# More up-projection pairs by seven products, and a longer plan, in a two-layer transformer trunk

## The chip, the core and the metric

The kernel runs on one core of one Trainium2 chip. A core has TensorE (PE in the profile; PEld is its weight load), VectorE (DVE), ScalarE (ACT), GpSimd (POOL) and SyncE (SP), which here only starts DMAs. Results of matmuls land in PSUM, which has eight banks of 128 partitions x 512 fp32 values; everything else lies in SBUF. GpSimd works on SBUF alone. The metric is the device time of one execution in microseconds (us).

## The reference

Two layers work on 512 tokens of width 1024 in fp32. Layer 0 mixes tokens by attention, layer 1 by a short convolution. Both go on with the same squared-ReLU MLP (hidden width 4096) and a gated embedding:

```python
for i in range(DEPTH):                                   # DEPTH = 2
    hn = rmsnorm(x, g[0])
    m = fox_attention(hn, ...) if i % 2 == 0 else short_conv(hn, ...)
    x = x + rmsnorm(m, g[1])
    h = rmsnorm(x, g[2])
    f = jnp.square(jax.nn.relu(h @ w_mlp_up[i])) @ w_mlp_down[i]
    x = x + rmsnorm(f, g[3])
    gate = jax.nn.sigmoid(rmsnorm(x, g[4]) @ w_ple_gate[i])
    x = x + rmsnorm((p[i] @ w_ple_proj[i]) * gate, g[5])
```

## The kernel before

**fp32 products.** Each operand is split into a high part (rounded to the matmul type, a cast on ACT) and a low part (value minus high part, a subtraction on DVE or POOL). `mm3` makes one product of three matmuls, high x high, low x high and high x low, at lines 420 to 422. A 512-column product is thus three matmuls of 512 columns. Of a weight tile `raw` the parts are named `wh` and `wl`.

**The MLP** (`mlp`) walks over eight groups of 512 hidden units. In each group four up-projections of 128 units (two *pairs*) are followed by a down-projection. Groups 0 to 6 do the down-projection by Strassen's scheme: a 2 x 2 block product by seven products instead of eight (`PRODUCTS`, in the order `STEPS`). Its operands are quarters of the activations (`A11`, `A12`, `A22` and the sums `S1` to `S4`, which POOL forms as tiles `s`) and quarters of the weights (`B11`, `B21`, `B22` and the sums `T1` to `T4`, tiles `dn_T`). Seven sums `acc` are carried over the groups, each group adding its products to them (`acc<-dn,acc`), and are combined after group 6. Group 7 has a plain down-projection.

**Up-projections by seven.** The pairs listed in `UP_SEVENS` use the same scheme, with 256-column matmuls: seven products of 12 matmuls (84) in place of 48 matmuls of 512 columns. They need sums of tokens (`T1` to `T4`, from the whole tokens `B..f`, once per layer), sums of weights (`up_S`, formed on POOL) and sums of the products (`d`, `v`, `m` on DVE). In the kernel before, these are the first pairs of groups 3 to 6.

**What sets the order.** Groups 1 to 6 of each MLP are laid out by a planner, `planned`: each step is put on an `Agenda` with an engine, a cost, what it follows, and the rooms it takes (raw weight buffers, banks). PE's order is written down; for ACT, DVE and POOL `emit` takes the ready step with the earliest due time, and the result is kept as the engines' order. Steps marked `shared` are planned one after the other with POOL's. Weights of a matmul may be split `LOOK` = 14 us before their use. Group 0, group 7 and everything outside the MLP are written as plain code (`up`, `down`, `combine`), weights being split some tiles ahead by `prepare`, and a scheduler orders them. Of the eight banks the planner gives 3 to the weight sums `dn_T` and 5 to products. The helper `add` at line 1208 issues all planned sums and low parts, so most DVE and POOL rows carry that line; line 1515 is the cast of a weight's high part.

Of the kernel before, what the change touches and what calls it, by code (L numbers as in the profile page):

```python
# [41 lines left out]
UP_SEVENS = [(gr, 0) for gr in range(3, 7)]  # L42
UP_FORMS = ("A11", "S2", "S1", "S3", "A12", "S4", "A22")
UP_PRODUCTS = (
    ("A11", "B11", "c", 0), ("S2", "T2", "a", 1), ("S1", "T1", "b", 0), ("S3", "T3", "b", 1),
    ("A12", "B21", "a", 0), ("S4", "B22", "c", 0), ("A22", "T4", "c", 1),
)
EXTRA = 7
LOOK = 14.0
LOOK_SUMS = 20.0  # L50
SUM_BANKS = 3
HOP = 0.25
MARGIN = 2.0
TOKENS_AT = 8.0
# [8 lines left out]
BANKED = range(1, 7)  # L63
# [17 lines left out]
low_on_pool = lambda key: key[0] == "up"  # L81


class Step:


    def __init__(self, engine, cost, run, after, begin, due, takes, uses, shared):
        self.engine, self.cost, self.run, self.shared = engine, cost, run, shared
        self.after, self.begin, self.due = list(after), begin, due
        self.takes, self.uses = takes, uses  # L90
        self.end = None


class Agenda:
# [5 lines left out]
    def add(self, engine, n, run, after=(), begin=0.0, due=1e9, takes=(), uses=(),  # L100
            shared=None):
# [3 lines left out]
                    engine == "POOL" if shared is None else shared)  # L105
# [5 lines left out]
    def emit(self):  # L111
# [8 lines left out]
        def room_for(step):  # L120
# [3 lines left out]
            for kind, n in need.items():  # L124
                left = self.rooms[kind] - n
# [56 lines left out]
def trunk(ctx: ExitStack, tc, x, xT, pT, g, gT, wv, wqk, bf, wo, wci, wcq, cw, wco, wup, wdn, wpp, wpg, out):  # L182
# [313 lines left out]
    def pre_norm(t, xs, gB, hT, name, also=lambda t, n, ps: None):  # L496
# [9 lines left out]

        put_off(t, turn)
# [601 lines left out]
    def mlp(l, hT, xs, then, late):  # L1109
# [72 lines left out]
        def planned(groups):  # L1182

            L, R, both = slice(0, S // 2), slice(S // 2, S), slice(0, S)
            agenda = Agenda({"raw": RAWS, "sum": SUM_BANKS, "ps": 8 - SUM_BANKS})
            first = begun[0]
            last = where["up", l, 14, 0] + SOON
# [10 lines left out]
            def act(n, run, after, uses=()):  # L1198
                return agenda.add("ACT", n, run, after, uses=uses)

            def dve(n, run, after, uses=(), due=1e9, shared=False):
                return agenda.add("DVE", n, run, after, uses=uses, due=due, shared=shared)
# [14 lines left out]

            def tokens_of_sevens():

                full = {}  # L1220
                for q in range(2):
                    for name in ("B11", "B12", "B22", "B21"):
# [8 lines left out]
                        full[name, q, 0] = gps(S, whole, (), begin=TOKENS_AT)  # L1231
                    for name, a, b in (("T1", "B12", "B11"), ("T2", "B22", "T1"),
                                       ("T3", "B22", "B12"), ("T4", "B21", "T2")):

                        def minus(name=name, q=q, a=a, b=b):
# [5 lines left out]
                        step = gps(S, minus, (full[a, q, 0], full[b, q, 0]))  # L1241
                        full[name, q, 0] = step
                        hi = act(S, lambda name=name, q=q: nc.scalar.copy(
                            T[name, q].hi[:, both], full[name, q][:, both]), (step,))
# [3 lines left out]
                            shared=True)  # L1248
# [10 lines left out]
            def part(gr, f, names, src, after, A):  # L1259
# [12 lines left out]
                step = dve(w, low, (act(w, high, (after,)),), shared=True)  # L1272
                for name in names:
                    low_of[gr, name, f // 2] = step

            def crossed(gr, f, q, at, A):

                d, m = (lambda: q["d"]), (lambda: q["m"])
                part(gr, f, ("A11", "A22"), lambda: q["d"][:, both], at["d"], A)
                part(gr, f, ("A12",), lambda: q["m"][:, R], at["m"], A)  # L1280
                sums(gr, f, q, at,
                     lambda: (q["m"][:, L], q["d"][:, R], q["d"][:, L], q["m"][:, R]), A)

            def sums(gr, f, q, at, of, A):
# [19 lines left out]
                a = gps(256, s12a, (at["d"], at["m"]))  # L1304
                b = gps(256, s12b, (a,))
                c = gps(256, s34a, (at["d"], at["m"]))
                e = gps(256, s34b, (b, c))
                part(gr, f, ("S1", "S2"), lambda: q["s12"][:, both], b, A)
                part(gr, f, ("S3", "S4"), lambda: q["s34"][:, both], e, A)

            def squared(gr, f, q, name, src, after, uses=()):

                def relu():
                    q["r" + name] = page(f"r{name}{l}_{gr}_{f}")
                    nc.scalar.activation(q["r" + name][:, both], src(), AF.Relu)
# [245 lines left out]
        def done(f, lo, hi, r):  # L1561
# [8 lines left out]
            if f == LATE:  # L1570
                gB.extend(late())
# [256 lines left out]
```

## Time and profile before

| | |
|---|---|
| median of 3 runs | 1214.74 us (1214.14 to 1214.89) |
| the profiled execution: time | 1214.68 us |
| its span, first to last instruction | 1212.9 us |
| granted TensorE clock | 0.999 |
| MLP of layer 0 / layer 1 in the span | 251.5 to 582.5 us / 817.7 to 1148 us |
| group 3 of layer 0 | 379 to 419 us |

The page's first part gives the busy time of each engine; the windows give the same for a stretch of the span, with the number of instructions behind x. In the views by group of instructions, "out<-in" names what is written and read, then come the count, the busy time, the mean duration of one in ns, and the engine's idle time ahead of them with what ended it. The chain of waits lists what released what, back from the last instruction: start, length, engine and line. PE's ends are modelled, so the pace of matmuls is read from starts.

### The profile page before, as it was taken

To read this page: it belongs to the slowest core of one execution; us is meant where nothing else is said; L and a number is where in the kernel's file an instruction comes from. 1 tells how busy PE (TensorE), PEld (TensorE's weight loads), DVE (VectorE), ACT (ScalarE), POOL (GpSimd) and SP (SyncE) were. 2 spreads that over 40 slices of the span, in tenths; PEclk is the share of its full clock that TensorE was granted. 3 is DMA by queue.
4 is the path that set the end of the run, shared out by engine and by line. 5 is a ranking of instruction groups with operands and counts; after the bars stand their busy time and mean duration, and the time that the engine had idled before them with its cause. 6 is when DMAs were issued, how large, how long until landed. Compare 5 with 4: busy or idle time off the path is not lost.

```text
span 1212.9 us, 19192 instructions
## 1 busy us (share of the span) xinstructions
PE 1201.4 (99%) x6463; PEld 1035.3 (85%) x6463; DVE 992.4 (82%) x1634; ACT 709.8 (59%) x1513; POOL 625.6 (52%) x592
## 2 busy tenths in 40 slices
PE   9999999999999999999999999999999999999997
PEld 7888887898888888888889999989888888888886
DVE  7888889584999999977877888766599999987773
ACT  7687778458664565445666533545757455663551
POOL 2035667155876765583213355226787567649110
PEclk9999999999999999999999999999999999999999
DMA  9475544623324333365223123542333334346301
GB/s 329 127 208 171 169 144 129 217 89 101 99 97 113 122 96 113 105 194 197 81 87 112 32 82 105 164 166 71 105 122 87 96 122 125 93 122 216 97 15 56
DMA packets 87316, 150.87 MB, mean 124 GB/s; under 512 B 10352, under 2 KB 18080, under 8 KB 87216
## 3 DMA queue, kind: packets, MB, share of 16 engines
q1 hardware_dynamic: 86640, 149.11, 39.5%
q8 instruction: 51, 0.84, 0.3%
q10 hardware_dynamic: 576, 0.53, 0.1%
q14 instruction: 49, 0.40, 0.1%
HBM read 139.03 MB, written 6.37 MB: 120 GB/s over the span
## 4 chain that ended last, share of the span: by engine, by line
PE 90%; DVE 3%; issue 2%; ACT 2%; POOL 1%; DMA 1%; SPq 0%; POOLq 0%; DVEq 0%; ACTq 0%
PE dn L420 8%; PE dn L422 8%; PE dn L421 8%; PE up L421 6%; PE up L420 6%; PE up L422 6%; PE v L628 3%; PE qk L420 2%; PE qk L422 2%; PE qk L421 2%; PE pg L420 2%; PE pg L421 2%; PE pg L422 2%; PE pT L742 1%; PE co L422 1%
## 5 line engine op out<-in xcount | busy, mean ns | idle before, releaser
L420 PE MATMUL up<-hTh,wh 128*128 128x512 f32 (+1 forms) x448 | 160.7, 359 | 0.0
L421 PE MATMUL up<-hTh,wl 128*128 128x512 f32 (+1 forms) x448 | 160.5, 359 | 0.0
L422 PE MATMUL up<-hTl,wh 128*128 128x512 f32 (+1 forms) x448 | 159.8, 359 | 0.0
L1208 POOL TENSOR_TENSOR wl<-raw,wh 128x512 fp32r<-128x512 f32 x88 | 137.6, 1590 | 27.0 <-ACT wh L1515 25.3
L429 DVE TENSOR_TENSOR wl<-raw,wh 128x512 fp32r<-128x512 f32 x162 | 140.5, 908 | 11.2 <-ACT wh L428 10.6
L1208 DVE TENSOR_TENSOR acc<-dn,acc 128x512 f32<-128x512 f32 x168 | 108.1, 679 | 6.4 <-PE dn L422 6.3
L428 ACT CAST wh<-raw 128x512 fp32r<-128x512 f32 x178 | 100.5, 628 | 4.5 <-DVE xd L525 4.4
L1515 ACT CAST wh<-raw 128x512 fp32r<-128x512 f32 x160 | 94.0, 620 | 2.4 <-DVE S3l L1208 2.4
L420 PEld LDWEIGHTS up<-hTh,wh 128*128 128x128 f32 x448 | 84.6, 189 | 12.4
L421 PEld LDWEIGHTS up<-hTh,wl 128*128 128x128 f32 x448 | 84.7, 189 | 12.1
L422 PEld LDWEIGHTS up<-hTl,wh 128*128 128x128 f32 x448 | 84.3, 189 | 12.6
L1515 ACT CAST wh<-dn_T 128x512 fp32r<-128x512 f32 x96 | 55.7, 585 | 64.3 <-DVE dn_T L1208 63.4
L1208 DVE TENSOR_TENSOR wl<-raw,wh 128x512 fp32r<-128x512 f32 x72 | 71.8, 1009 | 0.0
L1208 DVE TENSOR_TENSOR wl<-dn_T,wh 128x512 fp32r<-128x512 f32 x96 | 63.2, 680 | 1.4 <-ACT wh L1515 1.3
L1208 POOL TENSOR_TENSOR s<-qm,qd 128x256 f32<-128x256 f32 x8 | 6.9, 862 | 90.4 <-ACT qm L1319 71.1
L422 PE MATMUL qk<-hTl,wh 128*128 128x512 f32 x128 | 50.6, 396 | 0.0
L421 PE MATMUL pg<-wh,hTl 128*128 128x512 f32 x128 | 50.5, 394 | 0.0
L420 PE MATMUL pg<-wh,hTh 128*128 128x512 f32 x128 | 50.4, 394 | 0.0
L420 PE MATMUL qk<-hTh,wh 128*128 128x512 f32 x128 | 50.3, 393 | 0.0
L421 PE MATMUL qk<-hTh,wl 128*128 128x512 f32 x128 | 50.2, 392 | 0.0
L422 PE MATMUL pg<-wl,hTh 128*128 128x512 f32 x128 | 50.2, 392 | 0.0
L422 PE MATMUL dn<-wl,S3h 128*128 128x512 f32 x112 | 43.9, 392 | 0.1
(502 smaller groups left out, 4014.9 us busy)
## 6 DMA issues: line engine op xcount, KB each, us to landing
raw<-in_wup SPq DMA_DIRECT2D x128, 256.0 KB, 2.8
raw<-in_wdn SPq DMA_DIRECT2D x128, 256.0 KB, 2.7
raw<-in_wcq SPq DMA_DIRECT2D x36, 256.0 KB, 2.7
raw<-in_wqk SPq DMA_DIRECT2D x32, 256.0 KB, 5.3
raw<-in_wpg SPq DMA_DIRECT2D x32, 256.0 KB, 3.5
g<-in_g SPq DMA_DIRECT2D x22, 256.0 KB, 5.3
prl<-neg_c SPq DMA_DIRECT2D x16, 256.0 KB, 6.2
raw<-in_wo SPq DMA_DIRECT2D x16, 256.0 KB, 5.0
```

The lines of the kernel that those rows point to most:

```text
L420: nc.tensor.matmul(ps, a.hi, b.hi, start=start, stop=False)
L421: nc.tensor.matmul(ps, a.lo, b.hi, start=False, stop=False)
L422: nc.tensor.matmul(ps, a.hi, b.lo, start=False, stop=stop)
L428: nc.scalar.copy(hi, src)
L429: return eng.tensor_tensor(out=lo, in0=src, in1=hi.bitcast(F32), op=ALU.subtract)
L628: nc.tensor.matmul(ps[:, : V_CHUNKS[c][1]], getattr(of_x(k, t), p), getattr(ready["v", c, k], of), start=k == 0 and p == of, stop=k == KT ...
L742: nc.tensor.transpose(ps[:, b * P : (b + 1) * P], probs[h][b][:, j * P : (j + 1) * P], ident)
L1208: eng.tensor_tensor(out=out, in0=x, in1=y, op=op)
L1515: nc.scalar.copy(ready[key].hi[:, both], src())
```

## The change

1. `UP_SEVENS` lists both pairs of groups 2 to 6: ten pairs per layer by seven products, where there were four. The order of the seven products is A11, S2, A12, S1, S3, S4, A22.
2. The planner covers group 0, groups 1 to 6, the up-projections of group 7, and the splitting of all weights up to the gate's (`last` = four tiles before `pg`). `up_first` writes group 0 (for the first 128 units of each half of the tokens all matmuls with the tokens' high parts come first), `combined` puts the combining sums on POOL, `last_up` writes group 7's up-projections. Group 0's weight sums `dn_T` are formed on DVE in banks, where POOL formed them in SBUF.
3. For the weights of the down-projections and the sums `up_S` (`BESIDE`), ACT casts the value a second time, into a bank (`wb`). The low part is then the value minus `wb`, and no longer the value minus `wh`. 180 low parts read a bank so; the ACT casts grow by as many.
4. The products of a down-projection come in the order 1, 4, 2, 5, 6, 7, 3 (`TURNS`), no longer 1, 2, 4, 5, 6, 7, 3. Banks: 4 for weight sums and `wb` together, 4 for products. The planner also counts SBUF pages, and lets at most `IN_FLIGHT` = 14 split weights wait for PE.
5. The second pairs of groups 1 to 6 (where they go by seven) rectify and square the left half of `d` before the right half is there. Squares overwrite what they square.
6. `late`, the load of the residual and two gains, is issued 16 us of the plan before the down-projection of group 7.

The core of the diff:

```diff
-UP_SEVENS = [(gr, 0) for gr in range(3, 7)]
-UP_FORMS = ("A11", "S2", "S1", "S3", "A12", "S4", "A22")
+UP_SEVENS = [(gr, i) for gr in range(2, 7) for i in range(2)]
+UP_FORMS = ("A11", "S2", "A12", "S1", "S3", "S4", "A22")
...
+QUIET = 10.0
+IN_FLIGHT = 14
-SUM_BANKS = 3
+SUM_BANKS = 4
+APART_FROM = (1,)
+TURNS = (
+    (1, 0), (1, 1), (4, 0), (4, 1), (2, 0), (2, 1), (5, 0), (5, 1), (6, 0), (6, 1), (7, 0), (7, 1),
+    (3, 0), (3, 1),
+)
+BESIDE = ('dn', 'up_sum')
-TOKENS_AT = 8.0
+TOKENS_AT = 14.0
-BANKED = range(1, 7)
+BANKED = range(7)
...
-            last = where["up", l, 14, 0] + SOON
+            last = where["pg", l, 0, 0] + MORE
...
+                if i in APART_FROM and gr < 7:
+                    at["dl"] = squared(gr, f, q, "d", lambda: q["xd"], d, of=L)
+                    at["d"] = squared(gr, f, q, "d", lambda: q["xd"], e, of=R)
...
+                        def highs_first(ps=ps, of=of, weight=weight, f=f):
+                            ps.append(bank(f"up{l}_0_{f}{of.start}"))
+                            for k in range(KT):
+                                for part in ("hi", "lo"):
+                                    nc.tensor.matmul(
+                                        ps[0][:, L], weight(part, k), hT.hi[:, k, of],
+                                        start=k == 0 and part == "hi", stop=False,
+                                    )
...
+            up_first(A)
             tokens_of_sevens()
-            for gr in groups:
+            down_planned(0, A)
+            for gr in range(1, 7):
                 A = {}
                 for i in range(2):
                     (up_sevens if (gr, i) in UP_SEVENS else up_plain)(gr, i, A)
                 down_planned(gr, A)
+            combined()
+            blocks = [last_up(i) for i in range(2)]
...
+                def second_high(src=src, n=n, aside=aside):
+                    aside.append(bank(f"wb{n}"))
+                    nc.scalar.copy(aside[0].bitcast(F32R), src())
+
-                def low(key=key, src=src, eng=nc.gpsimd if plain_up else nc.vector):
-                    add(ready[key].lo[:, both], src(), ready[key].hi[:, both].bitcast(F32),
-                        ALU.subtract, eng)
+                def low(key=key, src=src, eng=nc.gpsimd if plain_up else nc.vector, aside=aside):
+                    of = aside[0] if aside else ready[key].hi[:, both].bitcast(F32)
+                    add(ready[key].lo[:, both], src(), of, ALU.subtract, eng)
...
+                if kind in BESIDE:
+                    hi = agenda.add("ACT", S, second_high, [hi], begin[0],
+                                    uses=uses, takes=[("sum", ("b", key))])
...
-                                         shared=not (of[0] == "dn" and isinstance(at, tuple)))
+                                         shared=kind != "dn_sum" and kind not in BESIDE)
```

**PE, the first pair of group 2 in layer 0.** `up0_2_0` is the bank of its first 128 units, `up0_2_0c` and `up0_2_0a` are banks of the pair by seven; `hTh` and `hTl` are the tokens' parts, `T2h` and `T2l` those of a token sum. Before:

```order
L420 MATMUL up0_2_0_4776<-hTh_87,wh113_4623 128x512
L421 MATMUL up0_2_0_4776<-hTh_87,wl113_4624 128x512
L422 MATMUL up0_2_0_4776<-hTl_88,wh113_4623 128x512
L420 MATMUL up0_2_0_4776<-hTh_87,wh113_4623 128x512
L421 MATMUL up0_2_0_4776<-hTh_87,wl113_4624 128x512
L422 MATMUL up0_2_0_4776<-hTl_88,wh113_4623 128x512
L420 MATMUL up0_2_0_4776<-hTh_87,wh114_4640 128x512
L421 MATMUL up0_2_0_4776<-hTh_87,wl114_4641 128x512
L422 MATMUL up0_2_0_4776<-hTl_88,wh114_4640 128x512
```

Now (the end of the first product and the start of the second, then the start of the third):

```order
L433 MATMUL up0_2_0c_4834<-hTh_87,wh112_4699 128x256
L434 MATMUL up0_2_0c_4834<-hTh_87,wl112_4700 128x256
L435 MATMUL up0_2_0c_4834<-hTl_88,wh112_4699 128x256
L433 MATMUL up0_2_0a_4857<-T2h0_0_4328,wh113_4826 128x256
L434 MATMUL up0_2_0a_4857<-T2h0_0_4328,wl113_4827 128x256
L435 MATMUL up0_2_0a_4857<-T2l0_0_4329,wh113_4826 128x256
L433 MATMUL up0_2_0a_4857<-hTh_87,wh114_4731 128x256
L434 MATMUL up0_2_0a_4857<-hTh_87,wl114_4732 128x256
L435 MATMUL up0_2_0a_4857<-hTl_88,wh114_4731 128x256
```

A weight tile served twelve matmuls of 512 columns, six for each of the pair's two blocks of units; now each of seven weight tiles serves twelve of 256 columns.

**DVE, the down-projection of group 3 in layer 0**, from the additions of its first product (`dn0_3_10`: product 1). Before:

```order
L1208 TENSOR_TENSOR acc0_1_0_4137<-dn0_3_10_5489,acc0_1_0_4137 128x512
L1208 TENSOR_TENSOR acc0_1_1_4139<-dn0_3_11_5490,acc0_1_1_4139 128x512
L1208 TENSOR_TENSOR dn_0_3_T3_0_5556<-dn_0_3_T2_0_5369,raw124_4970 128x512
L1208 TENSOR_TENSOR acc0_2_0_4163<-dn0_3_20_5520,acc0_2_0_4163 128x512
L1208 TENSOR_TENSOR acc0_2_1_4165<-dn0_3_21_5521,acc0_2_1_4165 128x512
L1208 TENSOR_TENSOR S1l0_3_2_5559<-s120_3_2_5518,S1h0_3_2_5558 128x512
L1208 TENSOR_TENSOR dn_0_3_T3_1_5584<-dn_0_3_T2_1_5454,raw126_5033 128x512
L1208 TENSOR_TENSOR acc0_4_0_4189<-dn0_3_40_5548,acc0_4_0_4189 128x512
L1208 TENSOR_TENSOR acc0_4_1_4191<-dn0_3_41_5549,acc0_4_1_4191 128x512
L1208 TENSOR_TENSOR wl154_5563<-dn_0_3_T3_0_5556,wh154_5562 128x512
L1208 TENSOR_TENSOR wl155_5599<-dn_0_3_T3_1_5584,wh155_5598 128x512
```

Now:

```order
L1243 TENSOR_TENSOR acc0_1_0_4174<-dn0_3_10_5739,acc0_1_0_4174 128x512
L1243 TENSOR_TENSOR acc0_1_1_4177<-dn0_3_11_5740,acc0_1_1_4177 128x512
L1243 TENSOR_TENSOR wl163_5735<-dn_0_3_T3_0_5685,wh163_5734 128x512
L1243 TENSOR_TENSOR A12l0_3_2_5791<-m0_3_1_5747,A12h0_3_2_5790 128x256
L1243 TENSOR_TENSOR S3l0_3_0_5751<-s340_3_0_5676,S3h0_3_0_5750 128x512
L1243 TENSOR_TENSOR acc0_4_0_4223<-dn0_3_40_5774,acc0_4_0_4223 128x512
L1243 TENSOR_TENSOR acc0_4_1_4232<-dn0_3_41_5775,acc0_4_1_4232 128x512
L1243 TENSOR_TENSOR S1l0_3_2_5826<-s120_3_2_5787,S1h0_3_2_5825 128x512
L1243 TENSOR_TENSOR acc0_2_0_4254<-dn0_3_20_5811,acc0_2_0_4254 128x512
L1243 TENSOR_TENSOR acc0_2_1_4258<-dn0_3_21_5812,acc0_2_1_4258 128x512
L1243 TENSOR_TENSOR wl164_5803<-dn_0_3_T3_1_5771,wh164_5802 128x512
L1243 TENSOR_TENSOR S3l0_3_2_5838<-s340_3_2_5799,S3h0_3_2_5837 128x512
```

Behind the additions of product 1 stand three instructions where one stood. Between the next pairs of additions stand one and two, where there were two and two. The products come in another order (1, 4, 2 where it was 1, 2, 4).

**POOL, group 0 of layer 0.** `s120` and `s340` are the sums `S1`/`S2` and `S3`/`S4` of a pair, `dn_0_0_T..` weight sums, `B..f` and `T..f` tokens and token sums. Before:

```order
L305 TENSOR_TENSOR dn_0_0_T1_1_3780<-raw81_3766,raw77_3758 128x512
L305 TENSOR_TENSOR dn_0_0_T3_1_3782<-raw83_3770,raw81_3766 128x512
L305 TENSOR_TENSOR dn_0_0_T2_1_3784<-raw83_3770,dn_0_0_T1_1_3780 128x512
L305 TENSOR_TENSOR dn_0_0_T4_1_3786<-raw79_3762,dn_0_0_T2_1_3784 128x512
L1141 TENSOR_TENSOR s340_0_0_3995<-q0_0_0_3751 128x256
L1141 TENSOR_TENSOR s120_0_1_4029<-q0_0_0_3751,q0_0_1_3752 128x256
L1141 TENSOR_TENSOR s120_0_1_4029<-s120_0_1_4029,q0_0_0_3751 128x256
L1141 TENSOR_TENSOR s340_0_0_3995<-q0_0_1_3752,s120_0_1_4029 128x256
L1141 TENSOR_TENSOR s340_0_2_4069<-q0_0_2_3753 128x256
L1141 TENSOR_TENSOR s120_0_3_4103<-q0_0_2_3753,q0_0_3_3754 128x256
L1141 TENSOR_TENSOR s120_0_3_4103<-s120_0_3_4103,q0_0_2_3753 128x256
L1141 TENSOR_TENSOR s340_0_2_4069<-q0_0_3_3754,s120_0_3_4103 128x256
```

Now:

```order
L1243 TENSOR_TENSOR B22f0_0_4043<-hTh_87,hTl_88 128x512
L1243 TENSOR_TENSOR T1f0_0_4068<-B12f0_0_3939,B11f0_0_3972 128x512
L1243 TENSOR_TENSOR s120_0_0_4091<-ql0_0_0_3793,qr0_0_1_3831 128x256
L1243 TENSOR_TENSOR s340_0_0_4111<-ql0_0_0_3793 128x256
L1243 TENSOR_TENSOR s120_0_0_4091<-s120_0_0_4091,ql0_0_0_3793 128x256
L1243 TENSOR_TENSOR B22f0_1_4136<-hTh_87,hTl_88 128x512
L1243 TENSOR_TENSOR s340_0_0_4111<-qr0_0_1_3831,s120_0_0_4091 128x256
L1243 TENSOR_TENSOR s120_0_2_4172<-ql0_0_2_3863,qr0_0_3_3965 128x256
L1243 TENSOR_TENSOR s340_0_2_4182<-ql0_0_2_3863 128x256
L1243 TENSOR_TENSOR s120_0_2_4172<-s120_0_2_4172,ql0_0_2_3863 128x256
L1243 TENSOR_TENSOR T1f0_1_4205<-B12f0_1_3990,B11f0_1_4012 128x512
L1243 TENSOR_TENSOR s340_0_2_4182<-qr0_0_3_3965,s120_0_2_4172 128x256
```

The weight sums of group 0 have left this queue, and token sums, which stood behind group 0's `s` sums, stand before and between them.

397 lines of the change are left out of this document (282 added, 115 removed).

## The prediction, blind

> **What bounds the kernel now.** I read the page's engine shares and its chain first, then the windows by group of the first MLP (with the sum line of the second), then a short window and two lines of the chain inside a group, to see what one matmul costs.
>
> ```profile
> span 1212.9 us, 19192 instructions
> PE 1201.4 (99%) x6463; PEld 1035.3 (85%) x6463; DVE 992.4 (82%) x1634; ACT 709.8 (59%) x1513; POOL 625.6 (52%) x592
> PE 90%; DVE 3%; issue 2%; ACT 2%; POOL 1%; DMA 1%; SPq 0%; POOLq 0%; DVEq 0%; ACTq 0%
> ```
> ```profile
> core 0: us, PE busy (x) PEld busy (x) DVE busy (x) ACT busy (x) POOL busy (x), PEclk, DMA share, GB/s
> 251.50:296.50 45.00, 44.84 (x294) 40.30 (x293) 28.85 (x37) 29.47 (x67) 25.16 (x25) 1.00 0.22 69
> 296.50:338.00 41.50, 41.45 (x182) 33.70 (x181) 34.32 (x41) 26.34 (x50) 38.13 (x31) 1.00 0.39 117
> 338.00:379.00 41.00, 41.00 (x182) 33.72 (x181) 40.65 (x53) 24.85 (x46) 34.71 (x26) 1.00 0.37 114
> 379.00:419.00 40.00, 40.00 (x218) 34.83 (x217) 39.03 (x56) 22.49 (x43) 25.94 (x21) 1.00 0.35 106
> 419.00:459.00 40.00, 40.00 (x218) 34.84 (x218) 39.14 (x57) 23.13 (x43) 24.54 (x19) 1.00 0.36 109
> ...
> 539.00:582.50 43.50, 43.50 (x194) 36.03 (x193) 30.95 (x42) 21.09 (x43) 19.70 (x18) 1.00 0.61 203
> sum 331.00, PE 330.79 PEld 283.09 DVE 285.55 ACT 191.01 POOL 217.90; mean PE 41.35 PEld 35.39 DVE 35.69 ACT 23.88 POOL 27.24
> ...
> sum 330.30, PE 330.27 PEld 283.15 DVE 284.21 ACT 190.32 POOL 217.95; mean PE 41.28 PEld 35.39 DVE 35.53 ACT 23.79 POOL 27.24
> ```
> ```profile
> 379.20:388.20 9.00, 9.00 (x77) 9.00 (x77) 8.18 (x13) 3.04 (x6) 3.21 (x2) 1.00 0.29 90
> ...
> 379.92 0.12 PE up_0c L422
> 337.27 0.23 PE dn L420
> 247.87 0.87 PE n_p L489 x8
> ```
> TensorE is the bound: 90% of the chain, at a granted clock of 1.00. A busy PE need not be a fast one, so its pace has to be checked. Inside a pair by seven products, 9.00 us hold 75 whole matmuls (77 less the two that the edges cut): 0.120 us from start to start at 256 columns, as in the chain. At 512 columns the chain has 0.23; closer, a group of one seven pair, one plain pair and its down-projection recurs every 40.0 us (379, 419, 459), and 40.0 - 84 x 0.120 = 29.9 us over 48 + 84 matmuls is 0.2267 us. So groups 3 and 4 are matmuls at full pace and nothing else: PE waits for nobody there, although DVE is busy 39.0 and 39.1 of 40.0 us. A whole MLP needs 192 x 0.12 (up, group 0) + 10 x 10.88 (plain pairs) + 4 x 10.08 (seven pairs) + 7 x 84 x 0.2267 (down) + 96 x 0.2267 (last down) + 16 x 0.11 (transposes) = 329.0 us, and takes 331.0 and 330.3. All that waiting could give back there is 3.3 us over both layers.
>
> **The change, part by part.**
>
> *Pairs by seven.* Four pairs per layer become ten, 12 more in all. A plain pair is 48 x 0.2267 = 10.88 us of PE, a seven pair 84 x 0.120 = 10.08 us: 0.80 us each, 12 x 0.80 = 9.6 us, all of it on the path. This is the main term. A rule speaks against it: the Trainium skill (TensorE: Matmul & The Clock Gate, Back-to-back issue gap) gives sustained spacings of about 81 ns at 128 columns and 131 ns at 512; an estimate half-way along for 256 columns is 98 ns, by which 84 short matmuls outlast 48 long ones and the change would cost some 23 us. The trace disagrees where it can be compared: 227 ns at 512 columns.
>
> *What DVE must do for it.* The order of the changed program has these DVE instructions from the first `acc` addition of one group to that of the next (512 columns / 256 columns): 52/3 from group 1 to 2, then 57/6, 55/6, 55/6, 52/6. Today it is 53/3 from group 3 to 4. The prices:
>
> ```profile
> L1208 DVE TENSOR_TENSOR acc<-dn,acc 128x512 f32<-128x512 f32 x74 | 47.7, 679 | 3.2 <-PE dn L422 3.2
> L1208 DVE TENSOR_TENSOR wl<-raw,wh 128x512 fp32r<-128x512 f32 x30 | 27.3, 917 | 0.0
> L1208 DVE TENSOR_TENSOR wl<-dn_T,wh 128x512 fp32r<-128x512 f32 x40 | 26.3, 680 | 0.7 <-ACT wh L1515 0.7
> L1208 DVE TENSOR_TENSOR wl<-up_S,wh 128x512 fp32r<-128x512 f32 x16 | 15.5, 981 | 0.0
> L1208 DVE TENSOR_TENSOR dn_T<-raw,dn_T 128x512 f32<-128x512 f32 x20 | 13.7, 687 | 0.7 <-ACT wh L1515 0.5
> ...
> L1208 DVE TENSOR_TENSOR A12l<-qr,A12h 128x512 fp32r<-128x512 f32 x6 | 6.8, 1128 | 0.1
> ...
> L1208 DVE TENSOR_TENSOR d<-up_0b,v 128x256 f32<-128x256 f32 x4 | 1.7, 417 | 0.0
> ```
> ```profile
> 323.07 1.20 DVE acc L1208 x2
> ...
> 333.31 3.41 DVE wl L1208 x2
> 336.72 0.04 issue
> 336.77 0.50 PE dn L422
> ```
> With one operand in a bank (`dn`, `dn_T`) an instruction takes 0.68 us. With both in SBUF it takes 0.92 to 1.13 us in the mean, and two of them 3.41 us in the chain, just ahead of a matmul that waits for them: GpSimd works on SBUF at the same time. Successive instructions overlap: two `acc` take 1.20 us, so one costs 0.60, and a 256-column one, less the same 0.08, 0.33. Group 3 to 4 today is then 53 x 0.60 + 3 x 0.33 = 32.8 us; the 39.1 us measured leave 6.3 us for its 20 SBUF-SBUF instructions, 0.32 us each. After the change the low parts of the `dn` weights and of the `up_S` sums read a copy in a bank, and only 11 SBUF-SBUF instructions are left (9 from group 1 to 2). DVE's need becomes 35.1 us from group 1 to 2, then 39.7, 38.5, 38.5 and 36.7, against PE's 2 x 10.08 + 19.04 = 39.2 us. One stretch is 0.5 us over, and it follows one with 4.1 us to spare in which weights can be made ahead (the plan lets them start 14 us early): no lasting lag. The low end of the added wait is 0, as today with DVE at 39.1 of 40.0. The high end takes the dearest row, 1128 - 680 = 0.45 us for each SBUF-SBUF instruction, and lets no lead count: needs of 41.2, 40.0 and 40.0 us, 3.6 us late per layer, 7.2 in all. I take 1.4 us, near the end that today's windows show.
>
> *Second roundings on ACT.* 14 more casts per group, into a bank, a write which the trace does not have. The nearest rows:
>
> ```profile
> L1515 ACT CAST wh<-raw 128x512 fp32r<-128x512 f32 x80 | 47.0, 620 | 1.2 <-DVE S3l L1208 1.2
> L1515 ACT CAST wh<-dn_T 128x512 fp32r<-128x512 f32 x48 | 27.9, 585 | 32.1 <-DVE dn_T L1208 31.7
> ```
> ACT gets 63 instructions per group for 43, of like shapes: 23.1 x 63/43 = 33.9 of 39.2 us. With the cast at 585 ns it is 0.5 us less. If the bank write doubled the cast, 14 x 0.6 = 8.4 us would bring ACT to 42 and cost up to 3 us a group; the two rows differ by 6% for the side that is read, so I take the same for the side that is written, no loss, and leave the upper end to rival C.
>
> *Banks.* Four for products instead of five. A down product holds two for 2.72 us of PE, and the product after next takes them, so its two `acc` additions (1.2 us) may come 1.5 us late. The tightest place in the changed order lies behind `acc` of product 1, where `wl`, `A12l` and `S3l` (1.53 + 2 x 0.32 = 2.2 us) stand before the next pair of `acc`: 1.2 + 2.2 + 1.2 = 4.6 us, within 2 x 2.72. It fits with 0.8 us.
>
> *Group 0.* Today's wait there follows GpSimd's sums for the second pair:
>
> ```profile
> 277.57 1.48 POOL s L1141 x2
> ...
> 279.11 1.08 POOL s L1141
> 280.22 0.63 ACT S1h L428
> 280.87 0.70 DVE S1l L429
> ...
> L1208 POOL TENSOR_TENSOR wl<-raw,wh 128x512 fp32r<-128x512 f32 x88 | 137.6, 1590 | 27.0 <-ACT wh L1515 25.3
> L1208 POOL TENSOR_TENSOR s<-qm,qd 128x256 f32<-128x256 f32 x8 | 6.9, 862 | 90.4 <-ACT qm L1319 71.1
> ```
> The change moves eight `dn_T` sums per layer from POOL to DVE (4.8 us, where DVE is busy 28.9 of 45.0) and puts token sums before the `s` sums on POOL, which may begin 14 us into the MLP: six of 1.59, three `s` of 0.86, one more of 1.59, four `s` of 0.86 end at 31.2 us. `S1h` and `S1l` (0.6 + 0.7) make 32.6. `S1` of the second pair is wanted by PE after 24.8 us of up work and 6 x 1.36 + 1.36 of down work, 34.3 us. It fits by 1.7 us, about a GpSimd instruction. Between no change and -3.3 us, I take -1.0.
>
> *Group 7 and the rest.* The last group's 14 `acc` sums on POOL (busy 19.7 of 43.5 us there) and the 12 `late` loads (DMA share 0.61) only start earlier. After the last up matmul come rectify, square, cast and subtraction, some 2.5 us; the PE order has 32 down matmuls (7.3 us) before the first that needs them. The transposes of the last tokens stand at the same place as today, 72 up matmuls in. Nothing for any of these.
>
> *Sum.* 1214.7 (the profiled execution: span 1212.9 and 1.8 around it; the median is 0.06 more) - 9.6 - 1.0 + 1.4 = 1205.5 us.
>
> **Rivals.**
> A. *DVE, or a bank behind it, is a little late in most groups.* The high end: 1214.7 - 9.6 + 7.2 = 1212.3; in part, 1208.5 to 1212.3. For it: needs of 94 to 101% of PE's time. Against it: 39.1 of 40.0 without a wait today.
> B. *Group 0 stops waiting altogether*: 1214.7 - 9.6 - 3.3 = 1201.8. For it: the 1.7 us to spare. Against it: one GpSimd instruction held up for the port takes that away.
> C. *Slower: a copy in a bank does not spare the rounding its wait.* Then 14 more instructions per group keep 0.32 us, 4.5 us; DVE needs 44.2, 43.0, 43.0 and 41.2 us, 14.6 us late per layer, 12.6 with the lead, so 1205.5 + 25 = 1230. It decides against the change from a loss of 1.3 us in each of these eight groups, that is, from DVE needs of 40.5 us. Against it: `dn_T<-raw,dn_T` has just these operands, SBUF first and a bank second, at 687 ns. A cast into a bank at twice its price would do the same through ACT.
> D. *Seven products are no saving where they are all that PE does.* Break-even is 10.88/84 = 0.1295 us per short matmul; at 0.15 us 12 x 1.7 = 20 us are lost instead of 9.6 gained: 1235. This would be the case of the skill's spacings above. The row with 75 in 9.00 us leaves it next to nothing.
>
> **How the numbers follow.** Forecast (1203.3 to 1208.5) 0.70; B 0.08; A in part 0.10; A in full or a beginning of C, within 0.2% of before (about what a measurement of this kernel can tell from no change: 1212.3 to 1217.2) 0.06; C 0.05; D 0.01. So faster 0.88, same 0.06, slower 0.06. The range 1202.5 to 1210.5 leaves out half of B and, above, 0.16: the dearer half of A in part and all that comes after it.
>
> **What would show it.** Right: 6,895 matmuls; seven pairs at 0.120 us a matmul; groups 2 to 6 following each other by 39.2 us; `wl<-raw,wb` and `wl<-up_S,wb` at about 680 ns; casts into `wb` near 600 ns; DVE busy 36 to 39.2 us in a group. Wrong: groups 40 us apart or more, with PE waiting for a `wl` or an `S` part from DVE, or for a bank (A, C); casts into `wb` above 1 us; a wait of over 1 us at group 0's `S` products (its term).

## The result, and the profile after

| | before | after |
|---|---|---|
| median | 1214.74 us (5 runs, 1214.14 to 1216.02) | 1208.99 us (5 runs, 1207.68 to 1210.76) |
| ratio, 95% interval | | 0.995 (0.9936 to 0.9963) |
| the profiled execution: time, span | 1214.68, 1212.9 us | 1207.68, 1206.0 us |

The forecast was 1205.5 us in a range of 1202.5 to 1210.5. The time lies in the range, 3.5 us above the forecast. The profiled execution is the shortest of the five; what is known of the other four is told at the end. The head, the chain and four groups of the page:

```profile
span 1206.0 us, 20586 instructions
PE 1191.4 (99%) x6895; PEld 1049.2 (87%) x6895; DVE 993.7 (82%) x1756; ACT 822.9 (68%) x1771; POOL 606.0 (50%) x612
...
PE 87%; DVE 5%; ACT 3%; issue 2%; DMA 1%; POOL 1%; POOLq 0%; ACTq 0%; DVEq 0%; SPq 0%
...
L1243 DVE TENSOR_TENSOR wl<-raw,wb 128x512 fp32r<-128x512 f32 x100 | 66.2, 676 | 5.8 <-ACT wb L1755 5.7
L1243 DVE TENSOR_TENSOR wl<-up_S,wb 128x512 fp32r<-128x512 f32 x80 | 52.8, 676 | 7.9 <-ACT wb L1755 7.9
L1755 ACT CAST wb<-raw 128x512 fp32r<-128x512 f32 x100 | 58.3, 590 | 0.0
L1755 ACT CAST wb<-up_S 128x512 fp32r<-128x512 f32 x80 | 46.9, 587 | 10.6 <-DVE acc L1243 10.2
```

TensorE is still the bound, but its share of the chain fell from 90 to 87% and DVE's rose from 3 to 5%. The 180 low parts that read a copy in a bank take 676 ns, the copies 587 to 590. The windows by group of the first MLP, then one group and the sum line of the second, show what DVE costs there:

```profile
core 0: us, PE busy (x) PEld busy (x) DVE busy (x) ACT busy (x) POOL busy (x), PEclk, DMA share, GB/s
251.10:295.10 44.00, 44.00 (x294) 40.58 (x294) 33.34 (x47) 37.25 (x82) 31.88 (x30) 1.00 0.31 97
295.10:335.90 40.80, 40.80 (x182) 33.78 (x181) 35.90 (x52) 29.65 (x58) 31.44 (x26) 1.00 0.29 92
335.90:375.10 39.20, 39.20 (x253) 35.88 (x252) 37.32 (x60) 32.14 (x65) 25.62 (x24) 1.00 0.32 103
375.10:414.40 39.30, 39.30 (x254) 35.99 (x253) 38.98 (x64) 31.14 (x64) 24.54 (x22) 1.00 0.35 110
...
532.10:575.80 43.70, 43.70 (x194) 36.18 (x194) 27.34 (x42) 26.51 (x54) 20.93 (x20) 1.00 0.68 227
sum 324.70, PE 324.70 PEld 290.16 DVE 284.25 ACT 248.10 POOL 209.33; mean PE 40.59 PEld 36.27 DVE 35.53 ACT 31.01 POOL 26.17
...
1017.40:1057.00 39.60, 39.51 (x254) 35.95 (x253) 38.14 (x62) 32.56 (x64) 24.87 (x23) 1.00 0.36 108
...
sum 324.80, PE 324.71 PEld 290.18 DVE 283.67 ACT 247.28 POOL 208.95; mean PE 40.59 PEld 36.27 DVE 35.46 ACT 30.91 POOL 26.12
```

Groups with two seven pairs last 39.2 to 39.3 us in the first MLP, with DVE busy 36.6 to 39.0 of them, and PE waits for nobody. In the second MLP one group of five lasts 39.6 us. Up to its first matmuls the chain runs mostly over DVE for 41 us (977.7 to 1019.2 us). About half of DVE's share of the whole chain lies there, yet PE loses only some 0.3 us: a share of the chain is not a loss. The MLPs fell from 331.0 and 330.4 to 324.7 and 324.8 us, 11.9 in all. The span fell by 6.9 only. PE's waits name what took the rest back; of these lines the trace before has one only (the last one here):

```profile
engine line waited for: us in total, times, longest us
PE c L434 <- DVE wl L442: 1.8, 2, 1.1
...
PE pg L435 <- DVE wl L442: 1.1, 2, 0.5
PE n0b_p L502 <- DVE n0b_h L493: 0.6, 1, 0.6
PE n_p L502 <- DVE n_h L493: 0.5, 2, 0.2
```
```profile
PE c L421 <- DVE wl L429: 0.3, 1, 0.3
```

All four of after lie behind an MLP: `n_p` (transposes of normed tokens) and `pg` (the gate's product) in both layers, `n0b_p` (transposes ahead of the convolution) and `c` (the convolution's first products) between the layers. Cutting each trace at the first `up` and the last `dn` matmul of each MLP gives its stages; here are those of seven profiled executions (us):

| run | to MLP 0 | MLP 0 | between | MLP 1 | behind | span |
|---|---|---|---|---|---|---|
| before | 251.5 | 331.0 | 235.2 | 330.4 | 64.8 | 1212.9 |
| after | 251.1 | 324.7 | 239.3 | 324.8 | 66.1 | 1206.0 |
| e1 old pairs | 250.8 | 329.9 | 239.4 | 329.9 | 66.0 | 1215.9 |
| e2 no copies in banks | 250.9 | 343.8 | 238.2 | 342.9 | 65.1 | 1240.9 |
| e7 two pairs alone | 250.9 | 338.6 | 235.2 | 338.2 | 64.8 | 1227.7 |
| e8 after, again | 251.8 | 324.5 | 240.7 | 326.1 | 66.0 | 1209.1 |
| e11 squares in turn | 252.2 | 324.6 | 236.7 | 325.5 | 65.9 | 1204.9 |

After against before: -0.4 ahead of the MLPs, -11.9 in them, +4.1 between them, +1.3 behind. The four waits account for these 5.4 us: laid beside the kernel before, start by start, PE falls back by some 1.3 us at `n_p` and `pg` in each layer, 1.0 at `n0b_p` and 2.0 at `c`. (The view lists less, 4.0 in all, since PE's ends are modelled.)

### The profile page after: what moved, and what is told of

It reads as the page before. It is cut to its first block, busy times and chain, and to the rows that moved or that the text cites. A ratio compares the mean times of both kernels' runs of the same rounds, so it can differ in the third digit from the quotient of the medians.

```text
span 1206.0 us, 20586 instructions
## 1 busy us (share of the span) xinstructions
PE 1191.4 (99%) x6895; PEld 1049.2 (87%) x6895; DVE 993.7 (82%) x1756; ACT 822.9 (68%) x1771; POOL 606.0 (50%) x612
## 3 DMA queue, kind: packets, MB, share of 16 engines
q1 hardware_dynamic: 86640, 149.11, 39.3%
## 4 chain that ended last, share of the span: by engine, by line
PE 87%; DVE 5%; ACT 3%; issue 2%; DMA 1%; POOL 1%; POOLq 0%; ACTq 0%; DVEq 0%; SPq 0%
PE dn L434 8%; PE dn L433 8%; PE dn L435 8%; PE up L433 3%; PE up L434 3%; PE up L435 3%; PE v L658 3%; PE qk L435 2%; PE qk L434 2%; PE qk L433 2%; PE pg L435 1%; PE pT L772 1%; PE pg L433 1%; PE pg L434 1%; PE o L435 1%
## 5 line engine op out<-in xcount | busy, mean ns | idle before, releaser
L442 DVE TENSOR_TENSOR wl<-raw,wh 128x512 fp32r<-128x512 f32 x130 | 97.4, 787 | 10.1 <-ACT wh L441 9.7
L1751 ACT CAST wh<-dn_T 128x512 fp32r<-128x512 f32 x112 | 65.1, 585 | 37.6 <-DVE dn_T L1243 37.1
L433 PE MATMUL up<-hTh,wh 128*128 128x512 f32 (+1 forms) x224 | 77.1, 344 | 0.0
L435 PE MATMUL up<-hTl,wh 128*128 128x512 f32 (+1 forms) x224 | 77.0, 344 | 0.0
L434 PE MATMUL up<-hTh,wl 128*128 128x512 f32 (+1 forms) x224 | 77.0, 344 | 0.0
L1243 DVE TENSOR_TENSOR wl<-raw,wb 128x512 fp32r<-128x512 f32 x100 | 66.2, 676 | 5.8 <-ACT wb L1755 5.7
L1751 ACT CAST wh<-up_S 128x512 fp32r<-128x512 f32 x80 | 49.6, 620 | 23.3 <-POOL up_S L1243 22.7
L1243 DVE TENSOR_TENSOR wl<-up_S,wb 128x512 fp32r<-128x512 f32 x80 | 52.8, 676 | 7.9 <-ACT wb L1755 7.9
L1755 ACT CAST wb<-raw 128x512 fp32r<-128x512 f32 x100 | 58.3, 590 | 0.0
L1243 POOL TENSOR_TENSOR up_S<-raw,raw 128x512 f32<-128x512 f32 x40 | 57.8, 1456 | 0.0
L1755 ACT CAST wb<-up_S 128x512 fp32r<-128x512 f32 x80 | 46.9, 587 | 10.6 <-DVE acc L1243 10.2
```

The lines of the kernel that those rows point to most:

```text
L433: nc.tensor.matmul(ps, a.hi, b.hi, start=start, stop=False)
L434: nc.tensor.matmul(ps, a.lo, b.hi, start=False, stop=False)
L435: nc.tensor.matmul(ps, a.hi, b.lo, start=False, stop=stop)
L442: return eng.tensor_tensor(out=lo, in0=src, in1=hi.bitcast(F32), op=ALU.subtract)
L1243: eng.tensor_tensor(out=out, in0=x, in1=y, op=op)
L1751: nc.scalar.copy(ready[key].hi[:, both], src())
```

## What each part is worth: three runs

**e1.** The changed kernel with the old seven pairs.

```diff
-UP_SEVENS = [(gr, i) for gr in range(2, 7) for i in range(2)]
+UP_SEVENS = [(gr, 0) for gr in range(3, 7)]
```

> The changed kernel with the old list of pairs by seven (first pairs of groups 3 to 6), everything else as changed. Theory: a pair by seven is worth its 0.80 us of PE and nothing else, so 12 pairs fewer add 9.6 us to the changed kernel's 1209.0: 1218 to 1219 us, that is 3 to 4 us slower than the kernel before, because the longer plan gains 2 us inside the MLPs and loses 5 us behind them. Rival: the loss behind the MLPs comes from the pairs (more work for DVE and ACT); then the rest of the change is a gain by itself and this gives about 1212.5 us, 2 us faster than before.

Measured: 1218.03 us (1217.31 to 1219.57), ratio to before 1.003 (1.0019 to 1.0041). The theory holds. By the table the twelve pairs are worth 5.2 + 5.1 = 10.3 us in the MLPs, for the 9.6 of the sum. Some 1.4 of the 10.3 are a wait of this run alone: group 6 lasts 40.7 us in each layer, for 40.0 before the change. Without the pairs the change loses 3 us: 1.6 gained in the MLPs, 5.4 lost between and behind them. So that loss belongs to the longer plan, not to the pairs.

**e2.** The changed kernel with no second roundings.

```diff
-BESIDE = ('dn', 'up_sum')
+BESIDE = ()
```

> The changed kernel without the second casts into banks: all low parts of weights read two SBUF operands again. Theory: 14 instructions per group pay 0.32 us more for the port shared with GpSimd, DVE needs 43 to 44 us in a group where PE needs 39.2, and PE waits 4 to 5 us in most of groups 2 to 5: about 25 us more than the changed kernel, 1230 to 1236 us, with PE waiting for wl and acc of DVE. Rival: ACT, which loses 14 casts per group (8 us), was as close to the limit as DVE, or the port waits fit into DVE's gaps: 1207 to 1213 us.

Measured: 1243.42 us (1242.23 to 1244.87), ratio 1.0235 (1.0219 to 1.025), 34 us more than the changed kernel, where 21 to 27 were expected. The windows of groups 2 and 4, and PE's first waits:

```profile
336.10:383.90 47.80, 43.83 (x254) 38.27 (x254) 47.13 (x67) 26.42 (x52) 31.61 (x25) 0.93 0.30 89
...
424.80:466.80 42.00, 40.91 (x253) 35.58 (x252) 41.62 (x62) 24.62 (x49) 29.06 (x23) 1.00 0.34 101
```
```profile
PE up_0a L434 <- DVE wl L1243: 5.2, 5, 2.3
PE dn L434 <- DVE A22l L1243: 4.8, 8, 0.8
```

DVE is busy 41.6 of 42.0 us in a group that needs 39.2 of PE: here it is the bound, as rival C had it. The low parts of `raw` and `up_S` weights take 1.03 to 1.16 us in the mean, for 0.68 with a copy in a bank. What was not expected is group 2: it takes 47.8 us, with DVE busy 47.1 of them. Four low parts of token sums (`T3l`, `T4l`, 4.8 us of DVE), which the changed kernel makes before this group, stand in it here. The granted clock of 0.93 there is hardly the cause: in layer 1 group 2 has a clock of 0.96 and takes 47.4. The edit does one thing more: the planner now plans these low parts one after the other with GpSimd's steps (`shared`). How much of the 34 us comes from that was not separated.

**e7.** The kernel before with two more pairs by seven.

```diff
-UP_SEVENS = [(gr, 0) for gr in range(3, 7)]
+UP_SEVENS = [(gr, 0) for gr in range(3, 7)] + [(5, 1), (6, 1)]
```

> The kernel before with the second pairs of groups 5 and 6 by seven products too, in the old plan and with no second roundings: 6,463 + 4 x 36 = 6,607 matmuls. Theory (the seven pairs are worth 0.80 us each only while DVE keeps up, and without the copies in banks it doesn't): groups 5 and 6 last 42 us instead of 40, as in the run without copies, 1220 to 1224 us. Rival (each pair is worth its 0.80 us in the old plan as well): 1214.7 - 3.2 = 1211.5 us.

Measured: 1229.74 us (1229.39 to 1231.04), ratio 1.0126 (1.0113 to 1.014). Four more seven pairs cost 15 us instead of saving 3.2. The sign is the theory's, but it gave 5 to 9 us: groups 5 and 6 last 43.1 and 44.8 us. PE's first waits, and two pieces of group 6:

```profile
PE dn L420 <- ACT A11h L1265: 5.4, 4, 1.4
PE dn L421 <- DVE A11l L1208: 4.7, 4, 2.1
```
```profile
522.00:526.00 4.00, 1.26 (x5) 0.47 (x3) 4.00 (x6) 3.34 (x7) 4.00 (x4) 1.00 0.65 204
526.00:530.00 4.00, 3.32 (x8) 2.65 (x9) 4.00 (x7) 0.62 (x1) 4.00 (x5) 0.60 0.44 134
```

The down-projection starts late for want of the quarter `A11`. Its last sum `d` comes out of the second pair's sums on DVE, and its low part stands there behind an `S3l` of 1.5 us; then PE runs at a clock of 0.60 for some 4 us (told at the end). So the seven pairs and what the change does around them need each other: the old plan with two pairs more per layer loses 15 us, the new plan with the old pairs loses 3, both together gain 6. Which of the change's other parts mends this (the copies in banks, the order of the products, the halves squared early) was not separated.

## Where the 5.4 us behind the MLPs come from: eight runs

The windows of group 7's up-projections and of the last down-projection, before and then after:

```profile
538.90:560.60 21.70, 21.70 (x97) 18.00 (x96) 14.75 (x16) 10.43 (x19) 16.55 (x12) 1.00 0.78 261
560.60:582.50 21.90, 21.90 (x98) 18.12 (x98) 16.30 (x26) 10.66 (x24) 3.24 (x6) 1.00 0.45 146
```
```profile
532.10:553.90 21.80, 21.80 (x97) 18.03 (x97) 8.34 (x12) 12.53 (x24) 17.82 (x14) 1.00 0.69 237
553.90:575.80 21.90, 21.90 (x98) 18.15 (x97) 19.00 (x31) 13.98 (x31) 3.11 (x6) 1.00 0.66 217
```

In the first stretch DVE's work fell from 14.75 to 8.34 us, in the second it rose from 16.30 to 19.00. In the plan the low parts of the last down-projection's weights begin 28.2 us ahead of the MLP's end, where they began 52.4 us ahead, and those that come behind the plan (`wl` L442: four of `pp`, then the gate's eight) can only follow them. Which rule of the plan holds the first ones back was not separated. Seven of the gate's eight were made before the first token block's additions; now five of them stand among its additions and its norm, where one stood. DVE's timeline there, before and then after (start, length; `acc<-dn` adds the last product, `xd` is the residual, `n_h` the normed block):

```profile
570.59 2.48 DVE L1583 TENSOR_TENSOR acc<-dn,acc 128x512 f32<-128x512 f32 x4 [2.90 <-PE dn L422]
572.99 1.31 DVE L518 TENSOR_TENSOR acc<-acc,g 128x512 f32<-128x512 f32 x2
574.22 0.74 DVE L525 SCALAR_TENSOR_TENSOR xd<-acc,mr_r_y,xd 128x512 f32<-128x512 f32 x1
...
578.12 1.42 DVE L480 SCALAR_TENSOR_TENSOR n_h<-xd,n_r_y,g 128x512 f32<-128x512 f32 x2 [0.27 <-POOL n_r_y L459]
```
```profile
563.62 0.69 DVE L1808 TENSOR_TENSOR acc<-dn,acc 128x512 f32<-128x512 f32 x1 [1.16 <-PE dn L435]
564.23 0.68 DVE L442 TENSOR_TENSOR wl<-raw,wh 128x512 fp32r<-128x512 f32 x1
564.83 0.69 DVE L1808 TENSOR_TENSOR acc<-dn,acc 128x512 f32<-128x512 f32 x1
565.43 1.28 DVE L442 TENSOR_TENSOR wl<-raw,wh 128x512 fp32r<-128x512 f32 x2
...
567.84 0.68 DVE L442 TENSOR_TENSOR wl<-raw,wh 128x512 fp32r<-128x512 f32 x1
...
570.24 1.40 DVE L555 SCALAR_TENSOR_TENSOR xd<-acc,mr_r_y,xd 128x512 f32<-128x512 f32 x2
...
573.97 1.42 DVE L493 SCALAR_TENSOR_TENSOR n_h<-xd,n_r_y,g 128x512 f32<-128x512 f32 x2
```

From the first addition to `xd` it was 3.6 us and is 6.6. The four blocks follow one another on DVE, so the delay reaches the last one. The start of each block's first `n_h`, from the end of its MLP (layer 0; layer 1 is the same within 0.3), with the time of the kernel:

| run | block 0 | 1 | 2 | 3 | median us |
|---|---|---|---|---|---|
| before | -4.4 | 2.1 | 9.3 | 15.9 | 1214.74 |
| after | -1.9 | 4.7 | 11.3 | 19.0 | 1208.99 |
| e5 | -4.6 | 4.4 | 11.0 | 18.9 | 1209.54 |
| e6 | -4.5 | 6.0 | 13.3 | 19.2 | 1214.44 |
| e9 | 0.2 | 8.2 | 17.0 | 22.3 | 1219.56 |
| e10 | 6.3 | 14.3 | 22.4 | 27.7 | 1227.53 |
| e11 | -4.7 | 2.5 | 9.9 | 16.3 | 1206.80 |

**e3.** The plan takes in the weights of `pp` too.

```diff
-MORE = -4
+MORE = 0
```

> The changed kernel with the plan reaching four weight tiles further (up to the gate's first): the four weights of the embedding's projection (pp) are split inside the plan, where before the change they were split during group 7. Theory: behind the plan 13 low parts (pp, pg) stand in DVE's queue between the last down-projection's results and the norm's steps (they took 7.8 us of the 21.9 us there) and make the norm of the first tokens 2.7 us late, which all later blocks inherit; four fewer make it 1 to 2 us earlier, the waits of PE before the gate's second half (0.4 and 0.7 us in each layer) go, and the time falls by 1 to 3 us, to 1206 to 1208. Rival: the order that the scheduler found there is what counts, not the number of splits: within 0.8 us of 1209.0, waits of another size at other places.

Measured: 1210.48 us (1207.89 to 1211.56), ratio 0.9959 (0.9945 to 0.9973). `n_p` and `pg` wait as long as without the edit. Four tiles more in the plan change nothing: their low parts stand at the same moments as without the edit (17.7 to 15.9 us ahead of the MLP's end), and the gate's eight still follow. A plan that takes in the gate's weights as well wasn't tried.

**e4.** The convolution's first weights are asked for four tiles earlier.

```diff
-                prepare(where["pg", l, 1, KT - 1] + 1 + SOON)
+                prepare(where["pg", l, 1, KT - 1] + 1 + SOON + 4)
```

> The changed kernel with four more weight tiles split ahead of the convolution's first projections (12 instead of 8 from the gate's fifth block on). Theory: the second half of the waits at the convolution's start (1.4 and 0.9 us of PE, released by low parts wl of DVE at 648 to 651 us) is due to these four splits standing behind the last norm in DVE's queue; split earlier they cost nothing, and 2 to 3 us go: 1206 to 1207 us. Rival: the norm's chain ends there anyway (hT of the last tokens), so the wait only changes its name: not more than 0.8 us.

Measured: 1210.94 us (1210.36 to 1212.6), ratio 0.9969 (0.9957 to 0.998). The rival holds: `c` no longer waits, but `n0b_p` now does, 4.0 us in one piece, and the time is no shorter. DVE's work is only put in another order there.

**e5 and e6.** The first block of the last down-projection asks for weights ten (e5) or six (e6) tiles ahead.

```diff
-                w = wide("dn", l, 7, n, f, soon=14)
+                w = wide("dn", l, 7, n, f, soon=14 if t else 10)
```

> The changed kernel, but the first token block of the last down-projection asks for weights only ten tiles ahead instead of fourteen, so that four of the gate's low parts stand on DVE behind that block's first norm and no longer among its additions. Theory (low parts that the plan no longer takes in delay the norm chain, and PE waits for the last tokens' transposes): the chain of the first tokens is about 2.5 us shorter, the waits of n_p and pg (1.1 to 1.3 us per layer) go, the waits for the convolution's weights stay: 1206.0 to 1207.5 us, or 1.5 to 3 us below the changed kernel run beside it. Rival (the chain is set by ACT, GpSimd and their hops, not by DVE's order): within 0.7 us of the changed kernel.

> As the run before, but six tiles ahead: all eight low parts of the gate's first weights stand behind the first block's norm on DVE, in the second block's. Theory: the first chain is as short, but eight low parts (4.8 us) now stand in the second block's chain, which is late in its place: the waits of n_p and pg return in part, 1206.5 to 1209 us. Rival (only the number of low parts between the last up-projection and the last norm counts): the same time as the changed kernel, 0.7 us either way.

**e8** is the changed kernel again, on the chip of e5 and e6.

> The changed kernel once more, as the measure for the two runs with the gate's weights moved: 1208 to 1210 us; at a granted clock of 0.999 about 1208, at 0.997 about 1209.5.

Measured: e5 1209.54 us (1208.73 to 1209.94), ratio 0.9957 (0.9943 to 0.997); e6 1214.44 (1211.85 to 1215.6), ratio 0.9998 (0.9989 to 1.0007); e8 1209.65 (1209.04 to 1210.93), ratio 0.9962 (0.9949 to 0.9974). My expectation of e5 fell. Block 0 is early again, as in the kernel before, but the four low parts then stood ahead of block 1's residual and between its halves, and blocks 1 to 3 are where they were. With eight there (e6) blocks 1 and 2 are 1.3 and 2 us later still, `pg` waits 2.4 us in one piece in each layer, the clock drops three times (told at the end), and the kernel is 5 us slower.

**e9 and e10.** DVE's order written out by hand: additions and gains of a block, then the norm of the block before, then the residual; weights ten (e9) or fourteen (e10) tiles ahead in the first block. (`streamed` counts columns of PE; the two lines around `then` keep the transposes at their places on PE.)

```diff
+        by_hand.enter_context(tc.manual_schedule(engines={mybir.EngineType.DVE}))
...
+            if t:
+                streamed[0] -= 24 * S
+                then(t - 1)
+                streamed[0] += 24 * S
             residual(t, mg, sums, xs[t], f"mr{l}")
-            then(t)
+        then(NB - 1)
```

> The changed kernel with DVE's order in the last down-projection written by hand: a token block's additions, gains and residual come ahead of every gate weight's low part that isn't needed yet (weights ten tiles ahead in the first block), and the next block's additions ahead of the norm of this one, so that DVE works while GpSimd forms the reciprocal root. Theory (DVE's late queue behind the plan is what costs 1.3 us per layer and, carried on through the gate, most of the 2.9 us at the convolution's first products): the last tokens' n_h comes near 17 us after the MLP instead of 19, n_p and pg no longer wait, and the waits at 646 to 651 us shrink: 1205 to 1207.5 us. Rival (only the waits of n_p and pg go, the convolution's stay): 1207 to 1208.5. Rival (another wait takes their place, as in the runs before): within 0.7 us of 1209.6.

> As the run before, but with weights fourteen tiles ahead in the first block as in the changed kernel: all the low parts of the gate's first weights stand ahead of the first additions on DVE, where the kernel before had them. Theory (what counts is that they are out of the norms' way): 0 to 1 us behind the run with the norms first, 1205.5 to 1208; DVE reaches the first additions about 1 us late, since ACT hands it the high parts one by one. Rival (only the order within the norms counts): the same time as that run.

Measured: e9 1219.56 us (1218.18 to 1220.02), ratio 1.0038 (1.0025 to 1.005); e10 1227.53 (1227.02 to 1228.03), ratio 1.0107 (1.0092 to 1.0123). Both expectations fell by more than 10 us, since the order itself made the norms later. In e9 the squares of block 1's sums (`junk<-acc`) stand ahead of those of block 0's residual (`junk<-xd`) on ACT, though the residual lay ready at 569.5; `n_h` waits for them. In e10 DVE stands 6.7 us before the last low part, for a high part that ACT makes late, and block 0's additions stand behind it:

```profile
572.55 0.63 ACT L477 ACTIVATE junk<-acc 128x512 f32<-128x512 f32 x1 [3.11 <-DVE acc L1810]
...
574.07 0.64 ACT L477 ACTIVATE junk<-xd 128x512 f32<-128x512 f32 x1
```
```profile
572.34 0.69 DVE L442 TENSOR_TENSOR wl<-raw,wh 128x512 fp32r<-128x512 f32 x1 [6.67 <-ACT wh L441]
572.95 1.28 DVE L1810 TENSOR_TENSOR acc<-dn,acc 128x512 f32<-128x512 f32 x2
```

They failed as improvements and serve as a test in the other direction: with later norms the kernel is longer.

**e11.** The order that these traces suggest, by hand on DVE and ACT: block t's additions, the squares and norm of block t-1, then block t's squares, gains and residual; two low parts behind each of the first two residuals, while GpSimd forms the reciprocal root.

```diff
+        by_hand.enter_context(tc.manual_schedule(engines={mybir.EngineType.DVE, mybir.EngineType.Activation}))
...
-                w = wide("dn", l, 7, n, f, soon=14)
+                w = wide("dn", l, 7, n, f, soon=0 if t else 10)
...
+            if t:
+                streamed[0] -= 24 * S
+                then(t - 1)
+                streamed[0] += 24 * S
             fs = [total[t, n][:, :S] for n in range(2)]
...
             residual(t, mg, sums, xs[t], f"mr{l}")
-            then(t)
+            if t < 2:
+                prepare(where["pg", l, 0, 0] + 6 + 2 * t)
+        then(NB - 1)
```

> The changed kernel with DVE's and ACT's orders in the last down-projection written by hand as the trace of the first such run suggests: the squares of a block's residual come ahead of the next block's squares on ACT, the next block's additions fill the wait for the reciprocal root on DVE, its gains stand behind this block's norm, and the last four low parts of the gate's first weights stand two by two behind the first two residuals. Theory (the time after the MLP follows the moment of the last block's norm, and the run with the norms first was slow because its own order put that at 22.6 us after the MLP): the norms come at about -4, 2.5, 9 and 16 us from the end of the MLP, n_p and pg wait for under 0.3 us, and of the 3 us at the convolution's first products up to 2.5 go: 1204.5 to 1207.5 us. Rival (the moment of the norm isn't what counts): 1209 or more.

Measured: 1206.80 us (1205.84 to 1206.99), ratio 0.9932 (0.9919 to 0.9946). This is the fastest of all kernels here, 2.8 us below the changed kernel in e8, the ranges apart. The two ran on different chips; against the kernel before on its own chip the ratios are 0.9932 here and 0.9962 in e8. The norms come within 0.9 us of the moments expected. PE's waits:

```profile
PE pg L434 <- DVE hTl L442: 1.7, 2, 0.9
...
PE c L434 <- DVE wl L442: 0.4, 1, 0.4
```

The waits of `n_p` and `n0b_p` are gone and that of `c` is 0.4. One point was missed: `pg` waits 0.9 us in each layer for another operand, the low part of block 1's transposed tokens, which stands behind block 3's gains on DVE. So the gain lies between the MLPs (239.3 or 240.7 to 236.7), and behind the second one nothing changed (65.9). No instruction was taken away, so what came back, 2.6 of the 5.4 us, was a matter of order on DVE and ACT. The other 2.8 us are still lost; the new waits of `pg` are in them.

## Why the prediction came out right, and which steps failed

By its own steps:

- *Pairs by seven, -9.6*: right. 10.3 by e1 against after, 1.4 of them a wait of e1's own; nine of the ten groups with two seven pairs recur every 39.2 to 39.3 us, and the 6,895 matmuls are there. Rival D is out, and with it the estimate of 98 ns from the Trainium skill (TensorE: Matmul & The Clock Gate, Back-to-back issue gap): the groups' 39.2 us hold 0.120 us per short matmul and 0.2267 per long one. (The 98 ns lie a third of the way from 81 to 131 ns, not half-way.)
- *DVE's need and the copies in banks, +1.4*: too dear. The prices were right (676 ns for some 680, 587 to 590 for near 600). Nine of the ten groups 2 to 6 last 39.2 to 39.3 us, no more than matmuls alone, the tenth 39.6. Rival A came true in small: in the nine traces with this plan and these pairs an MLP lasts 324.5 to 326.1 us, and what it is longer lies mostly in groups 4 and 5, where PE waits for DVE. DVE has no time to spare there. What rival C feared, low parts at the price of two SBUF operands, costs what it said or more, as e2 shows, but the copies prevent it.
- *Group 0, -1.0*: too small. Group 0 gave 1.0 and 0.5 us (45.0 to 44.0, 44.3 to 43.8), far from the 3.3 of rival B, and group 1, which I had put at nothing, 0.5 in each layer (41.3 to 40.8): 2.5 in all. The MLPs together gave 11.9 where the sum had 9.2.
- *Group 7 and the rest, "Nothing for any of these"*: this is the step that failed. The MLPs' surroundings lost 5.4 us. I had looked at what the change moves earlier (the sums on POOL, the loads) and not at what the end of the plan holds up: the splitting of the gate's weights, which had used DVE's idle time during group 7, comes behind the plan, and then stands in the way of the norms.

So 9.2 of gain were forecast, 6.9 came in the profiled execution and 5.75 by the medians: 2.7 more in the MLPs, 0.4 more ahead of them, 5.4 less behind them, and a clock that the sum did not hold. That the time lies in the range is in part luck: with the 9.2 us of the sum and the 5.4 lost it would be 1214.7 - 9.2 + 5.4 = 1210.9 us, outside. The 1209.0 us fall where the forecast had put rival A in part (1208.5 to 1212.3, 0.10), but lateness of DVE inside the groups is not what put them there.

## What to carry to other kernels

When a hand-made plan is extended, ask what used to slip into its idle time: work that is ordered after the plan piles up behind it, and the first chain there pays. A chain that goes round several engines (additions, squares, root, norm) is decided by the order on each of them; here a few low parts of 0.6 us in the first block's chain made the norms of all four blocks 2 to 3 us late. More matmuls of a cheaper kind paid here only because the engine that feeds them was relieved in the same change.

## What was not expected of the hardware

A wait of PE can cost more than its length. The windows at the convolution's first products, of after and then of e8, the same kernel with the same waits:

```profile
646.00:652.00 6.00, 3.50 (x26) 2.69 (x24) 5.71 (x8) 5.83 (x13) 4.34 (x4) 1.00 0.13 45
652.00:656.00 4.00, 4.00 (x36) 4.00 (x35) 4.00 (x6) 4.00 (x13) 2.22 (x2) 1.00 0.47 138
```
```profile
646.00:652.00 6.00, 3.60 (x26) 2.78 (x26) 5.27 (x7) 5.29 (x11) 4.25 (x5) 1.00 0.12 35
652.00:656.00 4.00, 4.00 (x22) 4.00 (x23) 4.00 (x6) 4.00 (x13) 2.64 (x2) 0.57 0.49 148
```

PE is idle for some 2.5 of 6 us in both. In e8 the granted clock then falls to 0.57 in the mean of 4 us, in which 22 matmuls start where after has 36, and the stage between the MLPs is 1.4 us longer. Cut where the drop begins and ends, the same trace shows half the clock for 3.41 us:

```profile
648.80:652.21 3.41, 1.57 (x12) 1.17 (x11) 3.41 (x4) 3.41 (x9) 3.33 (x3) 1.00 0.26 76
652.21:655.62 3.41, 3.41 (x19) 3.41 (x18) 3.41 (x6) 3.41 (x11) 2.43 (x2) 0.50 0.52 150
```

The profiled executions of after and e1 were spared, with the same waits. The other four of after show a mean clock of 0.997 instead of 0.999 and are 0.9 to 3.1 us longer. The profiled executions of e3, e5 and e8 show 0.997 too, and have the drop at this place; whether the four have it there can't be seen without their traces. In e11, where most of these waits are gone, no drop follows. In e7 four drops follow waits of 1.3 to 2.1 us for the quarter `A11`. At half the clock for 3.41 us each costs at most 1.7 us, an estimate, so the four explain up to 6.8 of the 18 us by which e7 misses its gain.

The Trainium skill (TensorE: Matmul & The Clock Gate, HAM oscillation) states that idle gaps above some 3.4 us bring the clock to half speed, and its Part 1 that the window by which this is judged runs freely. The traces agree with the half speed, with its length, and with a free-running window; but in e8 and e7 no single wait was as long as 3.4 us: waits of 0.5, 1.1 and 0.7 us within 5 us were enough.

The traces show what chance does here. Within one trace all drops begin whole multiples of 3.413 us apart: in e7 at 482.4, 526.8, 1055.8 and 1100.2 us, which is 13, 155 and 13 such steps. So each trace can be cut into stretches of 3.41 us on its own grid, and PE's idle time added up in each. In the thirteen traces, from 15 us on and while the clock was at 1.00, every stretch with 1.8 us or more of idle time was followed by a drop, and none with 1.4 us or less was; in between both occur. The two last waits of e8 fall into one stretch (1.8 us idle, the first of the two lines above), while in after and e1 the grid cuts the same waits so that no stretch holds more than 1.5 us.
